# Two value chunks of layer 1 as one Strassen stage, and accumulators that are taken over one by one

## The chip, the cores and the metric

The kernel runs on one core of one Trainium2 chip. The metric is the time of one execution on the device, in microseconds (us); lower is better. Engines are named as in the profile: PE (TensorE), DVE (VectorE), ACT (ScalarE), POOL (GpSimd), SP (SyncE, which here only issues DMAs).

## The reference

Two decoder layers on 256 tokens of width 2048, all in float32. "Layer 1" of the title is `l == 0` in the code: causal attention with 16 heads of 128. With 256 tokens there is one block of 256, so the block-sparse choice selects nothing. Layer 2 attends in a window of 128 with 4 shared K/V heads. Each layer ends with a gated feed-forward of width 5504. Cut to what matters:

```python
# layer 1
q, k, v = jnp.split(x @ w_qkv, 3, axis=-1)          # [256, 2048] @ [2048, 6144]
p = softmax(q k^T * 128**-0.5 + bias[t5_bucket(distance)], causal)   # per head
h = layer_norm(sqrt(2) * x + (p v) @ w_o)
# layer 2: the same with w_kv for 4 heads, w_q, a window of 128 and a learned sink in the softmax
# after each attention
g, u = jnp.split(causal_conv3(h @ w_up) + conv_b, 2, axis=-1)        # width 5504 each
h = layer_norm(sqrt(2) * h + (gelu(g) * u) @ w_down)
```

## The kernel before

**Products in three parts.** Each float32 operand is split into a high part (rounded to the PE's fast float32 form) and a low part (the rest). A product a·b is three matmuls, high·high, high·low and low·high, added in one PSUM bank.

**The weight stream.** All weights come as a list of "halves" of 128x1024 (512 KB), in the order in which PE uses them. SP loads half u into one of six `raw` buffers (L141). ACT makes the high part `wh` (L160), DVE the low part `wl` (L169), each with four buffers. `take` (L204) hands half i to PE and first splits half i+3, whose buffer becomes free when PE has done half i-1; the load of half i+9 is issued when DVE has split half i+3.

**Slots.** `step()` counts one slot for each half. `at(n, f)` puts work n slots ahead; it is issued to ACT, DVE, SP or POOL just before PE's matmuls of that slot and behind that slot's split. Each engine works in its program's order, so an instruction that waits holds up all behind it on that engine. All of the order in this kernel comes from these slots.

**Three ways to multiply.** `ws_unit` (L308) holds weights still and streams all 256 tokens; it makes one 128-wide feature block from two halves. `Moving.chunk` (L405) moves weights of 512 columns past two token tiles: one half is 2 blocks x 2 tiles x 3 = 12 matmuls of 512 columns. Mixed plans (`_mixed`, L62) do part of a projection by Strassen. A quad is 2 blocks of inputs (each 128) x 2 token tiles x 2 chunks of 512 columns; it takes seven products instead of eight. In the plan, `SEVEN` (L51) gives the halves of two quads: B11, B21, B22 are weight blocks, T1 to T4 are sums of weights. A mixed half is 2 products, 6 matmuls.

**Weight sums.** `presums` (L426) makes T1 to T4 ahead of use. For each quad SP loads 1 MB into `gb` in two parts (L433), DVE makes four sums of 128x512 (L436), POOL stores them to DRAM as `ws` (L440), and later they come back as `raw` halves. All quads share one area `gb`, so a quad's load waits for the sums of the quad before it. The first part is loaded in slot m, the second in m+1; the four sums run in slots m+4 to m+7.

**Input sums.** `sums(i)` (L582) makes the sums of inputs that the T halves need, for two quads at a time, in three steps on consecutive slots: `whole`, `combine`, `split` (L588, L599, L604/L605).

**PSUM.** There are eight banks: four named `acc`, four named `at`. In a mixed stage P1, P5, P6, P7 lie in `at`, the outputs (chunk n, token tile t) in `acc`. `evac` adds one output's bank into `res`; a bank can then be taken for another output. `fold` combines P1 to P7.

**Layer 1 attention, the first stage.** For each group g of four heads: the value chunk g (512 columns, `v_group`, 8 halves), then for each head a `ws_unit` for q and one for k, with that head's softmax in slots behind it. That is 4 x (8 + 16) = 96 slots. `project_out` with `PLAN_O` follows: chunks 0 and 1 with four quads (22 halves), chunks 2 and 3 plain (16 halves). `PLAN_DOWN` is the mixed plan of the feed-forward's second product.

**The bias.** The table of biases `ud` is spread into `band` in DRAM by `spread_bias` (L295; 512 KB in rows of 1 KB) and then loaded into `bias` by `load_bias` (L300, on POOL). For layer 1 the four spreads run on POOL, each followed by its load; for layer 2 they are issued by ACT.

Of the kernel before, what the change touches and what calls it, by code (L numbers as in the profile page):

```python
# [2 lines left out]

# [8 lines left out]
F32 = mybir.dt.float32  # L12
# [37 lines left out]
PLAINS_O = (5, 3, 0)  # L50
SEVEN = (("B11", "B21"), ("T1", "T3"), ("T2", "T4"), ("B22", "B22"), ("B11", "B21"), ("T1", "T3"), ("T2", "T4"))  # L51
# [28 lines left out]
ORDER = [q for li in range(4) for q in QUADS[li]]  # L80
AHEAD_OF = {0: QUADS[0] + QUADS[1][:8], 1: QUADS[1][8:] + QUADS[2], 2: QUADS[3][:4], 3: QUADS[3][4:]}
# [7 lines left out]
def _stages():  # L89

    for l in range(2):
        yield [None] * (48 if l else 96), 0
        yield PLAN_O, 2 * l
        yield [None] * (4 * FT), 0
        yield PLAN_DOWN, 2 * l + 1


@with_exitstack
def trunk(ctx: ExitStack, tc: tile.TileContext, wst, wsum, xT_in, x_in, relb, onehot, umask, sinks, conv_in, ln_g, ln_b, out):
# [195 lines left out]
    def spread_bias(l, h0, h1):  # L295
        a = ud[l, h0:h1, :]
        (nc.scalar if l else nc.gpsimd).dma_start(band[l, h0:h1], bass.AP(tensor=a.tensor, offset=a.offset + P - 1,
                                                    ap=[[UL, h1 - h0], [-1, P], [1, 2 * P]]))
# [127 lines left out]
    def presums(quads, first_slot, pitch):  # L426
# [18 lines left out]
        for i, q in enumerate(quads):  # L445
            m = first_slot + pitch * i
# [7 lines left out]
    def project_out(src, plan, li, homes, preload, turnover=None, quad_blocks=None):  # L454

        mv = Moving(src, 0)
        quads = bool(quad_blocks)  # L460
        p0, ns = (NH // 2 - NQ_O, 4) if li % 2 == 0 else (0, 3)
        w0 = nexth["i"] + len(plan) - WINDOW
        n0 = w0 + WINDOW
        after = homes is not None
        if not after:
            aside.update({w0 + j: (xT, j) for j in range(SPARE)})

        def settle():


            ring, places, following = homes()
            aside.update({w0 - len(ring) + j: x for j, x in enumerate(ring) if x})
            aside.update({w0 + j: x for j, x in enumerate(places)})
            aside.update({n0 + 4 + j: x for j, x in enumerate(following)})
            first = w0 - len(ring) - AHEAD
            for i in range(first, w0 + 3):
                reach[i] = i + min(AHEAD + (i - first) * 3 // 5, len(ring) - 1)
            for i, s in enumerate((4, 6, 7, 9, 11, 12, 13), w0 - 4):
                reach[i] = min(max(reach[i], w0 + s), n0 + 5)

        stats = stat.tile([P, 2, NCH, 6], F32, name="stats", bufs=1, padded_shape=[P, 2, NCH, 10])
        gb = gbp.tile([P, 2, D], F32, name="gb")

        def load_gb(i):
            a = (ln_g, ln_b)[i]
            (nc.sync if ns == 3 else nc.gpsimd).dma_start(gb[:, i], bass.AP(tensor=a.tensor, offset=a.offset + li * D, ap=[[0, P], [1, D]]))

        whole = sum(PLAINS[0]) + 7 * (NQ // 2)
        for i in range(2):
            if ns == 3:  # L490
                at((whole - 4, len(plan) - WINDOW - 5)[i], load_gb, i)
            else:
                load_gb(i)
        ag, rs = {}, {}
# [14 lines left out]
        def target(e):  # L509
# [3 lines left out]
            k1, k2, far = src(2 * k), src(2 * k + 1), xsum((k - p0) // 2, ns)  # L513
# [22 lines left out]

        def zs(t, n):
# [552 lines left out]
```

## Time and profile before

| what | value |
|---|---|
| median of 3 runs | 2053.36 us (2053.22 to 2055.54) |
| the profiled execution's own time | 2053.82 us |
| its span (first to last instruction) | 2052.1 us |
| PE busy | 2036.1 us, 99% of the span, 10908 matmuls |
| DVE busy | 1675.9 us, 82% |
| ACT busy | 1138.3 us, 55% |
| POOL busy | 75.4 us, 4% |
| DMA | 566.64 MB, mean 276 GB/s |
| mean granted PE clock | 0.998 |

Matmuls overlap: one of 512 columns lasts 389 ns, but the next starts about 227 ns after it, and that distance is what one costs. In the chain of work that ended last, PE has 98% of the span.

Stages of the profiled execution: group 0's value chunk starts at 5.1 us, group 2's at 151.8 us, group 3's at 225.0 us, layer 1's output projection at 298.3 us.

### The profile page before, as it was taken

The page shows a single profiled execution, that of the slowest core. Times are in us where ns is not written, and L with a number is a line of the kernel's source. Part 1 is how long each engine was busy: PE and PEld are TensorE (multiplying, and loading weights), DVE is VectorE, ACT ScalarE, POOL GpSimd, SP SyncE. Part 2 cuts the span into 40 slices and gives each one's busy share as a digit, 9 for nine tenths or more (in the row PEclk, how much of TensorE's full clock was granted, in tenths as well). Part 3 has the DMA queues.
Part 4 walks back from the last instruction along what each step waited for, and adds up shares of the span by engine and source line. Part 5 has one row for each costly group of instructions (what it writes and reads, how often), then busy time and mean ns, then how long its engine had stood idle before and what let it go on. Part 6 is the DMA issues. An engine that isn't in the chain of part 4 may idle for free.

```text
span 2052.1 us, 29718 instructions
## 1 busy us (share of the span) xinstructions
PE 2036.1 (99%) x10908; PEld 1759.3 (86%) x10908; DVE 1675.9 (82%) x2399; ACT 1138.3 (55%) x1676; POOL 75.4 (4%) x138
## 2 busy tenths in 40 slices
PE   9999999999999999999999999999999999999997
PEld 7888888988888888888888888898888888888886
DVE  5676678888888888899896788978888888889887
ACT  5444456455555555566673556545555555556672
POOL 0100000000000000000000000000000000000000
PEclk9999999999999999999999999999999999999999
DMA  8888988468888888888994767838888888889893
GB/s 297 287 281 328 320 287 313 162 238 282 289 288 273 282 296 269 285 286 329 323 366 156 261 217 252 285 126 275 281 286 283 279 283 291 272 266 328 312 361 150
DMA packets 158722, 566.64 MB, mean 276 GB/s; under 512 B 19008, under 2 KB 21376, under 8 KB 157296
## 3 DMA queue, kind: packets, MB, share of 16 engines
q1 hardware_dynamic: 136064, 492.74, 70.7%
q0 software_dynamic: 20160, 69.64, 8.7%
q10 hardware_dynamic: 2352, 2.36, 0.3%
q8 instruction: 86, 1.41, 0.3%
q14 instruction: 60, 0.49, 0.1%
HBM read 503.78 MB, written 65.06 MB: 277 GB/s over the span
## 4 chain that ended last, share of the span: by engine, by line
PE 98%; DVE 1%; DMA 0%; ACT 0%; issue 0%; ACTq 0%; DVEq 0%
PE acc L322 39%; PE acc L324 20%; PE acc L530 7%; PE acc L531 7%; PE acc L532 7%; PE at L532 2%; PE at L531 2%; PE at L530 2%; PE acc L386 2%; PE acc L385 2%; PE acc L387 2%; PE acc L349 1%; PE acc L361 1%; PE at L722 1%; PE at L755 1%; PE at L748 1%
## 5 line engine op out<-in xcount | busy, mean ns | idle before, releaser
L169 DVE TENSOR_TENSOR wl<-raw,wh 128x1024 fp32r<-128x1024 f32 (+1 forms) x754 | 898.8, 1220 | 186.4 <-ACT wh L160 163.9
L160 ACT ACTIVATE wh<-raw 128x1024 fp32r<-128x1024 f32 (+1 forms) x754 | 770.4, 1052 | 207.9 <-PE acc L532 104.5
L322 PE MATMUL acc<-xT,wh 128*128 128x512 f32 x3456 | 832.8, 392 | 0.0
L322 PEld LDWEIGHTS acc<-xT,wh 128*128 128x128 f32 x3456 | 641.1, 188 | 128.6
L324 PEld LDWEIGHTS acc<-xT,wl 128*128 128x128 f32 x3456 | 444.2, 190 | 12.4
L324 PE MATMUL acc<-xT,wl 128*128 128x256 f32 x3456 | 452.5, 284 | 0.0
L909 ACT ACTIVATE h<-acc 128x256 f32<-128x256 f32 x172 | 66.4, 386 | 409.1 <-PE acc L324 203.1
L917 DVE SCALAR_TENSOR_TENSOR c<-h,cw,c 128x255 f32<-128x255 f32 x344 | 165.4, 481 | 9.1 <-ACT c L913 2.8
L436 DVE TENSOR_TENSOR gb<-gb 128x512 f32<-128x512 f32 x224 | 153.5, 685 | 5.9 <-DMA gb<-in_wsum_dram 5.9
L910 DVE TENSOR_TENSOR h<-acc,h 128x256 f32<-128x256 f32 x172 | 72.7, 423 | 64.2 <-ACT h L909 64.2
L440 POOL DMA_DIRECT2D ws<-gb x112 | 59.8, 534 | 1412.1 <-DVE gb L436 1360.3
L530 PE MATMUL acc<-wh,up 128*128 128x512 f32 x275 | 107.0, 389 | 0.0
L531 PE MATMUL acc<-wl,up 128*128 128x512 f32 x275 | 107.0, 389 | 0.0
L532 PE MATMUL acc<-wh,up 128*128 128x512 f32 x275 | 107.0, 389 | 0.0
L913 ACT ACTIVATE c<-h,cw 128x256 f32<-128x256 f32 x172 | 101.7, 591 | 0.0
L530 PE MATMUL acc<-wh,st 128*128 128x512 f32 x174 | 68.8, 395 | 0.0
L531 PE MATMUL acc<-wl,st 128*128 128x512 f32 x174 | 67.8, 390 | 0.0
L532 PE MATMUL acc<-wh,st 128*128 128x512 f32 x174 | 67.8, 390 | 0.0
L831 ACT ACTIVATE qT<-acc 128x256 f32<-128x256 f32 x32 | 12.3, 385 | 91.3 <-PE acc L324 65.9
L532 PEld LDWEIGHTS acc<-wh,up 128*128 128x128 f32 x275 | 51.6, 188 | 10.7
L530 PEld LDWEIGHTS acc<-wh,up 128*128 128x128 f32 x275 | 51.6, 188 | 10.7
L531 PEld LDWEIGHTS acc<-wl,up 128*128 128x128 f32 x275 | 51.6, 188 | 10.6
(193 smaller groups left out, 2152.5 us busy)
## 6 DMA issues: line engine op xcount, KB each, us to landing
raw<-in_wst_dram SPq DMA_DIRECT2D x694, 512.0 KB, 5.2
gb<-in_wsum_dram SPq DMA_DIRECT2D x112, 512.0 KB, 7.6
ws<-gb POOLq DMA_DIRECT2D x112, 512.0 KB, 6.2
raw<-ws SPq DMA_DIRECT2D x112, 512.0 KB, 5.6
bias<-band POOLq DMA_DIRECT2D x8, 512.0 KB, 7.2
band<-ud POOLq DMA_DIRECT2D x4, 512.0 KB, 12.7
band<-ud ACTq DMA_DIRECT2D x4, 512.0 KB
res<-in_x_dram SPq DMA_DIRECT2D x2, 1024.0 KB, 9.4
```

Source lines behind the costliest of these rows:

```text
L160: nc.scalar.activation(wh[:, c], raws[s][:, c], AF.Copy)
L169: nc.vector.tensor_tensor(out=wl[:, c], in0=raws[s][:, c], in1=wh[:, c].bitcast(F32), op=ALU.subtract)
L322: nc.tensor.matmul(acc, w, xT[:, k, :], start=(k == 0), stop=(k == ends[0]))
L324: nc.tensor.matmul(acc[:, 0:T], w, xT[:, k, 0:T], start=False, stop=(k == ends[1]))
L436: nc.vector.tensor_tensor(out=w[:, o:o + 512], in0=a, in1=b, op=op)
L530: nc.tensor.matmul(acc, sh, wh, start=first, stop=False)
L531: nc.tensor.matmul(acc, sh, wl, start=False, stop=False)
L532: nc.tensor.matmul(acc, sl, wh, start=False, stop=last)
L909: nc.scalar.activation(h, acc[:, T:2 * T], AF.Copy)
L910: nc.vector.tensor_tensor(out=h, in0=acc[:, 0:T], in1=h, op=ALU.add)
L913: nc.scalar.activation(c, h, AF.Identity, bias=w[:, 3:4], scale=w[:, 2:3])
L917: nc.vector.scalar_tensor_tensor(c[:, d:T], h[:, 0:T - d], w[:, 2 - d:3 - d], c[:, d:T], op0=ALU.mult, op1=ALU.add)
```

## The change

1. The value chunks 2 and 3 are made together before group 2 (`v_pair`), by a mixed plan `PLAN_V` with four quads: 5 plain halves, 7 mixed, 3 plain, 7 mixed. Group 3 then has no chunk of its own. The functions of the mixed stages move out of `project_out` into `mixed`, unchanged.
2. The sums of these four quads are made first. Layer 1's attention starts its presums in slot 16 instead of 22 and makes 14 quads instead of 12, one each 6 slots, through the mixed stage too. The feed-forward of layer 1 makes 22 instead of 20, one each 7 slots instead of 8.
3. The bias spreads of layer 1 are issued in slots 4, 6, 8, 10 (before: 4, 9, 14, 19), the last three by ACT instead of POOL. Those of layer 2 move from slots 40, 47, 76, 82 to 76, 82, 88, 94.
4. In all mixed stages an output is evacuated when its own bank is complete, not when both token tiles of the chunk are.

```diff
+PLAN_V = _mixed(1, PLAINS_O, _plain(range(KB - 2 * NQ_O), (2, 3)), KB // 2 - NQ_O)
+QUADS[4] = [(4, 1, KB // 2 - NQ_O + p) for p in range(NQ_O)]
-AHEAD_OF = {0: QUADS[0] + QUADS[1][:8], 1: QUADS[1][8:] + QUADS[2], 2: QUADS[3][:4], 3: QUADS[3][4:]}
+AHEAD_OF = {0: QUADS[4] + QUADS[0] + QUADS[1][:6], 1: QUADS[1][6:] + QUADS[2], 2: QUADS[3][:4], 3: QUADS[3][4:]}
...
     def spread_bias(l, h0, h1):
-        (nc.scalar if l else nc.gpsimd).dma_start(band[l, h0:h1], ...
+        (nc.scalar if l or h0 else nc.gpsimd).dma_start(band[l, h0:h1], ...
...
             for n in range(NCH):
-                if n not in evacuated and done((n, 0), (n, 1)):
-                    evacuated.add(n)
-                    for t in range(2):
-                        at((t + 1) * (n % 2), evac, n, t)
+                for t in range(2):
+                    if (n, t) not in evacuated and done((n, t)):
+                        evacuated.add((n, t))
+                        at(t * (n % 2) * (ns == 3), evac, n, t)
...
-                at(4 + 5 * i, spread_bias, 0, h, h + 4)
-                at((40, 47, 76, 82)[i], spread_bias, 1, h, h + 4)
-            at((4 + 5 * i, 4 * i)[l], load_bias, bias, l, h, h + 4)
+                at(4 + 2 * i, spread_bias, 0, h, h + 4)
+                at((76, 82, 88, 94)[i], spread_bias, 1, h, h + 4)
+            at((5 + 2 * i, 4 * i)[l], load_bias, bias, l, h, h + 4)
...
+        def v_pair():
+            src = lambda k: xT[:, k, :]
+            k0 = KB - 2 * NQ_O
+            vts, begun = {}, set()
...
+            def into(t, n, a):
+                if n not in vts:
+                    vts[n] = pool.tile([P, 2, 512], F32, name="vt", bufs=2)
+                d = vts[n][:, t, :]
+                if (t, n) in begun:
+                    nc.vector.tensor_tensor(out=d, in0=d, in1=a, op=ALU.add)
+                else:
+                    begun.add((t, n))
+                    nc.scalar.activation(d, a, AF.Copy)
+
+            parted = mixed(src, PLAN_V, k0 // 2, 4, lambda i: xT[:, k0 + 4 * i:k0 + 4 * i + 4, :], place, into)
+            mv = Moving(src, 0)
+            for i in range(len(PLAINS_O) - 1):
+                for j, f in enumerate(parted.sums(i)):
+                    at(sum(PLAINS_O[:i]) + 7 * i + j, f)
+            evacuated = set()
+            for half in PLAN_V:
+                blocks = [mv.block() for _ in range(2)]
+                for e, w in zip(half, blocks):
+                    for tgt in parted.target(e):
+                        parted.product(*tgt, *w)
+                step()
+                for n in (2, 3):
+                    for t in range(2):
+                        if (n, t) not in evacuated and parted.done((n, t)):
+                            evacuated.add((n, t))
+                            at(0, lambda n=n, t=t: into(t, n, parted.banks.pop((n, t))))
+            parted.fold(1)
+            run(before)
+            return vts
...
-        presums(AHEAD_OF[2 * l], 3 if l else 22, 8 if l else 6)
+            presums(ahead, [16 + 6 * i for i in range(len(ahead))])
...
-                vt = v_group()
+                if g < 2:
+                    vt = v_group()
+                elif g == 2:
+                    vts = v_pair()
+                if g >= 2:
+                    vt = vts[g]
...
-            presums(AHEAD_OF[2 * l + 1], 4, 8)
+            presums(AHEAD_OF[2 * l + 1], range(4, 158, 8 if l else 7))
```

How the instructions stand, at three places.

DVE before, in the third value chunk (`st` is head outputs, `L` a head's logits, `gb` a weight sum):

```order
L761 TENSOR_TENSOR st<-at,st 128x256
L726 SCALAR_TENSOR_TENSOR L<-at,bias 128x128
L728 TENSOR_REDUCE nm<-L 128x1
L726 SCALAR_TENSOR_TENSOR L<-at,bias 128x256
L728 TENSOR_REDUCE nm<-L 128x1
L169 TENSOR_TENSOR wl<-raw,wh 128x1024
L436 TENSOR_TENSOR gb<-gb 128x512
```

DVE in the changed kernel, from the first mixed group of the pair into the second (`tmp` and `st` are the input sums):

```order
L443 TENSOR_TENSOR gb<-gb 128x512
L176 TENSOR_TENSOR wl<-raw,wh 128x1024
L443 TENSOR_TENSOR gb<-gb 128x512
L176 TENSOR_TENSOR wl<-raw,wh 128x1024
L533 TENSOR_TENSOR tmp<-xT 128x1024
L176 TENSOR_TENSOR wl<-raw,wh 128x1024
L544 TENSOR_TENSOR tmp<-tmp 128x2x128 x4
L176 TENSOR_TENSOR wl<-raw,wh 128x1024
L443 TENSOR_TENSOR gb<-gb 128x512
L550 TENSOR_TENSOR st<-tmp,st 128x1024
L176 TENSOR_TENSOR wl<-raw,wh 128x1024
L443 TENSOR_TENSOR gb<-gb 128x512
```

The weight sums of other quads now stand between the splits of the mixed halves, and one stands ahead of the input sums' last step. In all, four weight sums stand between the split of half 11 and that of half 15, and a fifth ahead of L550.

DVE before, at the end of the mixed part of layer 1's output projection (the `xT` and `up` tiles are here buffers of split weights):

```order
L605 TENSOR_TENSOR xT<-tmp,xT 128x1024
L169 TENSOR_TENSOR wl<-raw,wh 128x1024 x2
L169 TENSOR_TENSOR xT<-raw,xT 128x1024 x3
L169 TENSOR_TENSOR up<-raw,up 128x1024
L549 SCALAR_TENSOR_TENSOR res<-res,acc 128x512
L169 TENSOR_TENSOR up<-raw,up 128x1024
L549 SCALAR_TENSOR_TENSOR res<-res,acc 128x512
L169 TENSOR_TENSOR up<-raw,up 128x1024
L169 TENSOR_TENSOR wl<-raw,wh 128x1024
L549 SCALAR_TENSOR_TENSOR res<-res,acc 128x512 x2
```

The same place in the changed kernel:

```order
L550 TENSOR_TENSOR xT<-tmp,xT 128x1024
L176 TENSOR_TENSOR wl<-raw,wh 128x1024
L613 SCALAR_TENSOR_TENSOR res<-res,acc 128x512
L176 TENSOR_TENSOR wl<-raw,wh 128x1024
L176 TENSOR_TENSOR xT<-raw,xT 128x1024 x2
L613 SCALAR_TENSOR_TENSOR res<-res,acc 128x512
L176 TENSOR_TENSOR xT<-raw,xT 128x1024
L176 TENSOR_TENSOR up<-raw,up 128x1024
L613 SCALAR_TENSOR_TENSOR res<-res,acc 128x512
L176 TENSOR_TENSOR up<-raw,up 128x1024 x2
L176 TENSOR_TENSOR wl<-raw,wh 128x1024
L613 SCALAR_TENSOR_TENSOR res<-res,acc 128x512
```

The first two evacuations move ahead by four to five splits. The banks that they free are those that chunk 2 takes.

SP before, from the end of the inputs' loads to the second quad:

```order
L233 DMA xc<-in_xT_dram 128x512
L141 DMA raw<-in_wst_dram 128x1024 x23
L433 DMA gb<-in_wsum_dram 128x1024
L141 DMA raw<-in_wst_dram 128x1024 x2
L433 DMA gb<-in_wsum_dram 128x1024
```

SP in the changed kernel:

```order
L240 DMA xc<-in_xT_dram 128x512
L148 DMA raw<-in_wst_dram 128x1024 x17
L440 DMA gb<-in_wsum_dram 128x1024
L148 DMA raw<-in_wst_dram 128x1024 x2
L440 DMA gb<-in_wsum_dram 128x1024
```

The first quad's load stands six halves earlier. In the program's semaphores that load now also waits for the landing of the third bias spread that ACT issues, since DMAs of SP and ACT take eight semaphores in turn; before, no load up to slot 40 waited for a spread.

More of the change, by code (lines that the diff above doesn't have):

```diff
@@ L444, in presums @@
                  (1536, b21, w[:, 1024:1536], ALU.subtract))
-        for i, q in enumerate(quads):
-            m = first_slot + pitch * i
+        for m, q in zip(slots, quads, strict=False):
             at(m, load, q, 0)
@@ L452, in presums, with mixed @@
                     at(m + 4 + j, store, q, j // 2)
[L454 to L494, printed above, removed]
+    def mixed(src, plan, p0, ns, quad_blocks, place, into):
         banks, used, owed = {}, {}, {}
@@ L607, in sums, with project_out, settle, load_gb @@
             return whole, combine, split
+        return SimpleNamespace(banks=banks, target=target, product=product, done=done, fold=fold, sums=sums)
+    def project_out(src, plan, li, homes, preload, turnover=None, quad_blocks=None):
+        mv = Moving(src, 0)
+        quads = bool(quad_blocks)
+        p0, ns = (NH // 2 - NQ_O, 4) if li % 2 == 0 else (0, 3)
+        w0 = nexth["i"] + len(plan) - WINDOW
+        n0 = w0 + WINDOW
+        after = homes is not None
+        if not after:
+            aside.update({w0 + j: (xT, j) for j in range(SPARE)})
+        def settle():
+            ring, places, following = homes()
+            aside.update({w0 - len(ring) + j: x for j, x in enumerate(ring) if x})
+            aside.update({w0 + j: x for j, x in enumerate(places)})
+            aside.update({n0 + 4 + j: x for j, x in enumerate(following)})
+            first = w0 - len(ring) - AHEAD
+            for i in range(first, w0 + 3):
+                reach[i] = i + min(AHEAD + (i - first) * 3 // 5, len(ring) - 1)
+            for i, s in enumerate((4, 6, 7, 9, 11, 12, 13), w0 - 4):
+                reach[i] = min(max(reach[i], w0 + s), n0 + 5)
+        stats = stat.tile([P, 2, NCH, 6], F32, name="stats", bufs=1, padded_shape=[P, 2, NCH, 10])
+        gb = gbp.tile([P, 2, D], F32, name="gb")
+        def load_gb(i):
+            a = (ln_g, ln_b)[i]
+            (nc.sync if ns == 3 else nc.gpsimd).dma_start(gb[:, i], bass.AP(tensor=a.tensor, offset=a.offset + li * D, ap=[[0, P], [1, D]]))
+        whole = sum(PLAINS[0]) + 7 * (NQ // 2)
+        for i in range(2):
+            if ns == 3:
+                at((whole - 4, len(plan) - WINDOW - 5)[i], load_gb, i)
+            else:
+                load_gb(i)
+        ag, rs = {}, {}
+        def zs(t, n):
+            return res[:, t, n * 512:(n + 1) * 512]
+        parted = mixed(src, plan, p0, ns, quad_blocks, lambda i: xsum(i, ns), lambda t, n, a: into(t, n, a))
+        banks, target, product, done, fold, sums = (parted.banks, parted.target, parted.product, parted.done, parted.fold,
+                                                    parted.sums)
+        paired = {e[2] for half in plan for e in half if e[0] == "B11"}
+        parts = {(t, n): 1 + (2 if (t, n % 2) == (1, 1) else 1) * (n // 2 in paired) for t in range(2) for n in range(NCH)}
+        scaled = set()
+        def into(t, n, a):
+            z = zs(t, n)
+            if (t, n) in scaled:
+                nc.vector.tensor_tensor(out=z, in0=z, in1=a, op=ALU.add)
+            else:
+                nc.vector.scalar_tensor_tensor(z, z, ALPHA, a, op0=ALU.mult, op1=ALU.add)
+                scaled.add((t, n))
+            parts[t, n] -= 1
+            if not parts[t, n]:
+                nc.vector.bn_stats(stats[:, t, n, :], z)
+        def evac(n, t):
+            into(t, n, banks.pop((n, t)))
```

52 lines of the change are left out of this document (27 added, 25 removed).

## The prediction

> **What bounds the kernel now.** I read the page first: its busy line and the chain of work that ended last.
>
> ```profile
> PE 2036.1 (99%) x10908; PEld 1759.3 (86%) x10908; DVE 1675.9 (82%) x2399; ACT 1138.3 (55%) x1676; POOL 75.4 (4%) x138
> PE 98%; DVE 1%; DMA 0%; ACT 0%; issue 0%; ACTq 0%; DVEq 0%
> ```
>
> PE is the bound almost everywhere. So only two things can shorten the time: fewer matmuls, or the few waits that PE still has. All others can only lengthen it, by making PE wait where it doesn't now. The view of waits, for PE:
>
> ```profile
> PE acc L530 <- DVE res L549: 1.0, 2, 0.5
> PE acc L530 <- DVE res L547: 0.8, 2, 0.4
> PE acc L386 <- DVE wl L169: 0.7, 2, 0.5
> ```
>
> The columns are total us, times, longest. The first two rows are the waits of mixed stages for an evacuation (L547, L549), which the change touches. The third lies in value chunks.
>
> What one matmul costs comes from PE's timeline in the third value chunk, which the change replaces:
>
> ```profile
> 173.41 0.39 PE L385 MATMUL acc<-wh,xT 128*128 128x512 f32 x1
> ...
> 175.91 0.39 PE L387 MATMUL acc<-wh,xT 128*128 128x512 f32 x1
> ```
>
> Eleven matmuls start within 2.50 us: 0.227 us from start to start.
>
> **Part 1, fewer matmuls.** The chunks 2 and 3 have 16 plain halves of 12 matmuls, 192. The pair has 8 plain (96) and 14 mixed of 6 (84), 180. Twelve less, times 0.227: **-2.72 us**, all on PE's path.
>
> **Part 2, one-by-one evacuation.** PE's timeline at the four waits: first the output projection of layer 1, then the first product with `PLAN_DOWN`, then the two of layer 2.
>
> ```profile
> 342.14 0.39 PE L532 MATMUL acc<-xT,st 128*128 128x512 f32 x1
> 343.02 0.50 PE L530 MATMUL acc<-xT,st 128*128 128x512 f32 x1 [0.50 <-DVE res L549]
> ...
> 344.07 0.40 PE L531 MATMUL acc<-xT,st 128*128 128x512 f32 x1
> ```
>
> ```profile
> 982.90 0.39 PE L532 MATMUL acc<-wh,st 128*128 128x512 f32 x1
> 983.67 0.47 PE L530 MATMUL acc<-wh,xT 128*128 128x512 f32 x1 [0.38 <-DVE res L547]
> ...
> 984.44 0.40 PE L530 MATMUL acc<-wh,xT 128*128 128x512 f32 x1
> ```
>
> ```profile
> 1294.27 0.50 PE L530 MATMUL acc<-xT,st 128*128 128x512 f32 x1 [0.49 <-DVE res L549]
> ```
>
> ```profile
> 1934.87 0.47 PE L530 MATMUL acc<-wh,xT 128*128 128x512 f32 x1 [0.38 <-DVE res L547]
> ```
>
> From 342.14 to 344.07 are 1.93 us for five matmuls, 1.14 at their usual distance: 0.80 lost, more than the 0.50 in brackets, since the starts after it are wider apart too. From 982.90 to 984.44 are 1.54 for four (0.91): 0.63. The two of layer 2 have the same brackets, so they count the same: 2 x (0.80 + 0.63) = **-2.86 us**. I take all of it, because the bank that chunk 2 takes is freed four to five splits earlier in the new order of DVE, over 4 us by the 1.14 us of a split (below), and the waits were under 1 us. Bounds: 0, if another bank is late instead, and -2.86. Work late next there is none that PE's waits show.
>
> **Part 3, the pair as a mixed stage with weight sums under it.** This stage has no like in the profile: the output projection is the same plan, but its mixed halves have no weight sums beside them. I take its times and add the sums. PE starts half 5, the first mixed one, here:
>
> ```profile
> 314.37 0.48 PE L530 MATMUL at<-wh,st 128*128 128x512 f32 x1
> ```
>
> Call it T0. From there to half 16 stand seven mixed halves (42 matmuls), three plain (36) and one mixed (6): 84 x 0.227 = 19.07 us. The low part of the second group's input sums is used two matmuls later, at T0 + 19.52 = 333.89. DVE, in three pieces of its timeline:
>
> ```profile
> 294.89 2.36 DVE L169 TENSOR_TENSOR wl<-raw,wh 128x1024 fp32r<-128x1024 f32 x2
> 297.16 0.69 DVE L436 TENSOR_TENSOR gb<-gb 128x512 f32<-128x512 f32 x1
> 297.76 1.22 DVE L169 TENSOR_TENSOR wl<-raw,wh 128x1024 fp32r<-128x1024 f32 x1
> ```
>
> ```profile
> 319.86 6.67 DVE L169 TENSOR_TENSOR wl<-raw,wh 128x1024 fp32r<-128x1024 f32 x5
> 326.44 1.22 DVE L588 TENSOR_TENSOR tmp<-st 128x1024 f32<-128x1024 f32 x1
> ```
>
> ```profile
> 328.02 1.23 DVE L169 TENSOR_TENSOR wl<-raw,wh 128x1024 fp32r<-128x1024 f32 x1 [0.36 <-ACT wh L160]
> ...
> 331.97 1.23 DVE L605 TENSOR_TENSOR xT<-tmp,xT 128x1024 fp32r<-128x1024 f32 x1
> ```
>
> A weight sum costs 297.16 to 297.76, 0.60 us; a split 1.14 (2.36 - 1.22). L605 is done at 333.20, 0.69 before it is needed. In the pair five weight sums stand between the split of half 11 and L605's like: 3.0 us. DVE has room for some of it: the five splits and what follows take 326.44 - 319.86 = 6.58, of which 5 x 1.14 = 5.70 is work, so 0.88 is free, and 0.36 before 328.02. So L605's like comes 3.0 - 0.88 - 0.36 = 1.76 late, less the 0.69 of room: PE waits **1.1 us**. This is what happens if no load is late.
>
> The loads of the weight sums may be. In this stage a half lasts 1.36 us (6 x 0.227) and not the usual 3, so the quad's two loads and its sums lie closer together. Its second part can be issued when DVE has read the same area for the quad before, in my estimate at T0 + 2.6 (behind the split of half 8, which lies between 312.03 and 317.14 in the stage before); the second sum, which reads it, comes behind the split of half 12, at about T0 + 8.3 (319.86 + 2 x 1.14 + 0.60 = 322.7). That leaves 5.7 us for the load. The view of L433 says how long such loads take before:
>
> ```profile
> DMA to landing us min/median/max: 4.4/7.6/10.6
> ```
>
> So DVE waits 0, 1.9 or 4.9 us more, and PE with it: 1.1, 3.0 or 6.0 in all. I take the median, **+3.0**. Lower bound 0: DVE's other work (the stage before also carries the end of a head's softmax) is less than in the row I borrowed from.
>
> The whole stage moves 22 raw halves, 8 loads and 7 stores of weight sums (37 x 0.524 MB) and 1.05 MB of residual: 20.4 MB in the 44 us that the output projection's mixed part takes, 464 GB/s. The best that a window of the profile shows, with the next term's:
>
> ```profile
> 180.00:185.00 5.00, 5.00 (x39) 4.72 (x38) 3.40 (x5) 2.28 (x3) 0.53 (x1) 1.00 1.03 427
> 500.00:600.00 100.00, 100.00 (x576) 88.25 (x575) 84.12 (x132) 55.30 (x90) 4.80 (x9) 1.00 0.83 278
> ```
>
> The last column is GB/s. At 427 the stage's bytes take 47.8 us, 3.8 more than the stage; the ring of loaded halves, which was filled before, is six deep (over 8 us of mixed halves) and covers that, so I count nothing beyond the late loads above. The Trainium skill, "DMA: Bandwidth & Descriptors", section "Where 436 GB/s comes from", says that between HBM and SBUF the HBM side binds, at about 358 GB/s for each core; by it the stage takes 57 us, 13 more than it has, which would leave a PE wait of some 4 us beyond the ring, by my estimate. The row of 427 disagrees, and the measurement decides.
>
> **What I cost at nothing.** The six more halves to load and split, and the 14th quad, lie under PE in layer 1's attention. The feed-forward of layer 1 gets two quads more, 8 sums of 0.69 = 5.5 us of DVE over some 400: in the second window row DVE (third pair) is busy 84 of 100, PE 100. The layer 2 spreads move between slots; SP has waited for them all the same, without any wait of PE there:
>
> ```profile
> SPq L141 <- DMA band<-ud: 16.1, 3, 7.5
> ```
>
> If that cover goes (a wait of over 9 us, three halves of the ring), PE stops. The value tiles' evacuation (ACT, then DVE additions) runs behind the pair, and the units after it take banks freed at halves 15 and 19. ACT is held at slot 6 until `ud` has landed, 28.22 in the next fence, and then issues three spreads; its splits for the first `q` unit come about 3 us later, and it had this much free (3.99 before 35.41):
>
> ```profile
> 35.41 0.38 ACT L831 ACTIVATE qT<-acc 128x256 f32<-128x256 f32 x1 [3.99 <-PE acc L324]
> ```
>
> **Sum.** -2.72 - 2.86 + 3.0 = -2.6. The profiled execution's own time is 2053.82 (its span 2052.1 and 1.7 around it), 0.46 above the median of the runs, 2053.36. So 2051.2 for such an execution, 2050.8 against the median; I say **2051.0**. A difference under 0.2% (4.1 us) can't be told from no change here, so the forecast itself is "same".
>
> **Rival 1, slower: the spreads at the start.** POOL's queue, then the view of L297 for POOL's spreads, and DVE's and the chain's rows where the first sum would stand:
>
> ```profile
> 28.22 1.12 POOL L297 DMA_DIRECT2D band<-ud  x1 [4.44 <-DMA ud<-us]
> 41.51 0.79 POOL L301 DMA_DIRECT2D bias<-band  x1 [12.17 <-DMA band<-ud]
> ```
>
> ```profile
> DMA to landing us min/median/max: 11.5/12.7/14.0
> ```
>
> ```profile
> 66.07 0.42 DVE L832 TENSOR_TENSOR kT<-acc,kT 128x256 f32<-128x256 f32 x1 [1.43 <-ACT kT L831]
> 67.45 2.36 DVE L169 TENSOR_TENSOR wl<-raw,wh 128x1024 fp32r<-128x1024 f32 x2 [0.96 <-ACT wh L160]
> ```
>
> ```profile
> 72.85 0.23 PE acc L322
> 73.08 1.92 PE acc L324 x16
> ```
>
> The first sum's load (slot 16) waits for ACT's third spread to land, and all raw loads stand behind it on SP. Its sum (slot 20) stands ahead of the splits of 67.45, whose result PE needs at 73.08: it can start at 73.08 - 0.69 - 1.22 = 71.2 at the latest. A load that finds the queues empty lands in about 6 (between 4.4 and 7.6), so the third spread must have landed by 65.2. If ACT's spreads begin at 28.8 and run one after the other, that allows 12.1 us each; at 11.5 there's no wait, at 12.7 one of 1.7, at 14.0 one of 5.6. The issues of the same spread by ACT later in the profile, under weight sums, speak for longer: one issued at 146.31 still held SP at 169.18, 22.9 us:
>
> ```profile
> 146.31 0.61 ACTq L297 DMA_DIRECT2D band<-ud  x1
> ```
>
> ```profile
> 169.18 0.90 SPq L141 DMA_DIRECT2D raw<-in_wst_dram  x2
> ```
>
> Against it: at the start no weight sums load the queues. At 15 us each, nearest to the 14.0, the wait is 28.8 + 45 + 6 - 71.2 = 8.6: **2059.6**; it is slower by more than 0.2% (over 2057.5) from 14.3 us each. By the Trainium skill, the same page, section "Why a DMA increments its semaphore by 16 and not by 1", a transfer whose slowest dimension has 4 steps, as a spread's four heads, uses 4 DMA engines, and on ACT's queue always the lowest-numbered, which would put the three spreads on the same four. The 12.7 beside 7.6 for a weight load of the same bytes agrees with the first; no row here shows the second.
>
> **Rival 2, no gain: loads late at their worst.** The 10.6 above: +6.0, so 2053.4 + 0.4 = **2053.8**. The 464 GB/s asked of a peak of 427 speak for it, the ring against it.
>
> **Rival 3, faster: DVE keeps up.** No wait in the pair: -5.6, **2047.8**. For it, the softmax work that isn't in the pair; against it, the five sums that stand where only 1.9 us is free.
>
> **How the numbers follow.** Forecast 0.40 (2049.0 to 2052.5), rival 1 0.25, rival 2 0.15, rival 3 0.20. Faster by over 0.2% is below 2049.2: rival 3, and a seventh of the forecast, 0.26. Slower is above 2057.5: two thirds of rival 1, 0.17. The rest, 0.57, is the same. The range: rival 3's end, 2047.5, to rival 1's price, 2059.6; what lies above has about 0.1 (the longer spreads of rival 1), below 0.08.
>
> **What would show it.** Right: 10896 matmuls; no PE wait at the four places for L547/L549's like; one PE wait of 1 to 6 us at half 16's `T1` product on the input sums' last step, with DVE waiting for `gb` behind half 12's split. Rival 1: a wait of PE for a split near 73 us, SP held until about 74 by a spread. Rival 2: PE waits for splits within the pair on raw loads. Wrong altogether: a wait of PE in a place I have costed at nothing, above all in the feed-forward or under layer 2's spreads.

## The result, and the profile after

The changed kernel takes 2068.38 us (median of 6 runs, 2067.24 to 2069.11) against 2053.98 for the kernel before in the same series. The ratio is 1.0069, 95% interval 1.0056 to 1.0082: 14 us slower. The forecast was 2051.0, which can't be told from no change, with a range that ended at 2059.6; a slower kernel had been given a chance of 0.17. The prediction was wrong.

The page's busy line and chain. The line numbers are those of the changed kernel: L160/L169 of before are L167/L176 here, L530 to L532 are L496 to L498, and L605 is L550.

```profile
PE 2038.4 (99%) x10896; PEld 1759.7 (85%) x10896; DVE 1701.1 (82%) x2441; ACT 1147.4 (56%) x1685; POOL 76.5 (4%) x143
PE 91%; DVE 3%; DMA 3%; issue 1%; ACTq 0%; ACT 0%; SPq 0%; DVEq 0%
```

The twelve matmuls are gone, but the chain now leaves PE for 9% of the span. PE's waits:

```profile
PE acc L331 <- DVE wl L176: 6.0, 2, 4.8
PE at L498 <- DVE st L550: 4.1, 1, 4.1
...
PE at L496 <- ACT st L549: 1.2, 1, 1.2
...
PE at L497 <- DVE wl L176: 0.6, 2, 0.3
```

To size the losses I add up, along PE's timeline, how much farther apart matmuls start than matmuls of the same shapes usually do. That counts waits and slow starts behind them alike, and it closes: the span grew by 13.4 us (2065.5 - 2052.1), and

| place | before | after | change |
|---|---|---|---|
| near 41 to 49 us, first heads | 0 | 7.28 | +7.28 |
| the pair, 196 to 229 us | 0 | 10.48 | +10.48 |
| two output projections, evacuation | 1.53 | 0 | -1.53 |
| two down projections, evacuation | 1.24 | 1.12 | -0.12 |
| twelve matmuls | | | -2.72 |

Nothing else changed by more than tenths. The sizes depend by some tenths on what is taken as the usual distance, and each comes from one profiled execution.

**The start.** ACT's timeline, and PE's at the loss. An ACTq row with a long time is an issue that holds the engine:

```profile
27.85 1.19 ACTq L304 DMA_DIRECT2D band<-ud  x1
29.16 1.06 ACT L167 ACTIVATE wh<-raw 128x1024 fp32r<-128x1024 f32 x1 [3.57 <-issue]
29.19 8.84 ACTq L304 DMA_DIRECT2D band<-ud  x1
...
38.24 8.72 ACTq L304 DMA_DIRECT2D band<-ud  x1
...
47.06 2.00 ACT L167 ACTIVATE wh<-raw 128x1024 fp32r<-128x1024 f32 x2 [6.68 <-issue]
```

```profile
35.54 1.12 PE L331 MATMUL acc<-xT,wl 128*128 128x256 f32 x8
41.42 1.79 PE L331 MATMUL acc<-xT,wl 128*128 128x256 f32 x8 [4.76 <-DVE wl L176]
```

The second and third spread each held ACT almost 9 us. The splits behind them came late, DVE's low parts behind those, and PE waited 4.76 us in the middle of a unit.

**The pair.** PE's timeline:

```profile
194.59 0.39 PE L498 MATMUL acc<-wh,xT 128*128 128x512 f32 x1
196.19 0.50 PE L496 MATMUL at<-wh,st 128*128 128x512 f32 x1 [1.20 <-ACT st L549]
196.52 0.40 PE L497 MATMUL at<-wl,st 128*128 128x512 f32 x1
201.00 0.79 PE L498 MATMUL at<-wh,st 128*128 128x512 f32 x1 [4.08 <-DVE st L550]
201.59 0.63 PE L496 MATMUL at<-wh,st 128*128 128x512 f32 x1
...
205.43 0.50 PE L496 MATMUL acc<-wh,st 128*128 128x512 f32 x1
```

This is the place that was forecast, the low part of the second group's input sums, but PE waits 4.1 us and not 3. Behind it ten matmuls take 4.43 us (201.00 to 205.43) instead of 2.27: PE's granted clock is a half there. The windows of the pair, the last columns PEclk, DMA share, GB/s:

```profile
180.00:190.00 10.00, 10.00 (x46) 8.29 (x45) 8.12 (x10) 6.14 (x6) 0.53 (x1) 1.00 0.99 376
190.00:200.00 10.00, 5.71 (x24) 4.08 (x23) 6.78 (x10) 4.83 (x6) 0.53 (x1) 0.94 1.02 418
200.00:210.00 10.00, 9.01 (x30) 7.27 (x31) 8.95 (x10) 5.00 (x7) 1.07 (x2) 0.72 1.00 351
210.00:220.00 10.00, 8.76 (x54) 7.69 (x53) 6.14 (x8) 5.35 (x8) 0.55 (x2) 1.00 1.01 392
220.00:230.00 10.00, 9.56 (x50) 7.93 (x50) 9.90 (x15) 2.28 (x3) 0.52 (x1) 1.00 1.02 418
```

The DMA engines are busy all the time for 50 us, at 391 GB/s on the mean. Ahead of PE's two waits stand ACT, which waits for a raw load, and DVE, which waits for a load of weight sums:

```profile
194.13 1.06 ACT L167 ACTIVATE wh<-raw 128x1024 fp32r<-128x1024 f32 x1 [3.90 <-DMA raw<-ws]
```

```profile
199.11 0.69 DVE L443 TENSOR_TENSOR gb<-gb 128x512 f32<-128x512 f32 x1 [2.66 <-DMA gb<-in_wsum_dram]
```

So one trace allows two readings: DVE held by a late `gb` load, or every load late. The experiments tell them apart.

### The profile page after: what moved, and what is told of

Same layout as the page of the kernel before. It is cut to its first block, busy times and chain, and to the rows that moved or that the text cites. A ratio compares the mean times of both kernels' runs of the same rounds, so it can differ in the third digit from the quotient of the medians.

```text
span 2065.5 us, 29824 instructions
## 1 busy us (share of the span) xinstructions
PE 2038.4 (99%) x10896; PEld 1759.7 (85%) x10896; DVE 1701.1 (82%) x2441; ACT 1147.4 (56%) x1685; POOL 76.5 (4%) x143
## 4 chain that ended last, share of the span: by engine, by line
PE 91%; DVE 3%; DMA 3%; issue 1%; ACTq 0%; ACT 0%; SPq 0%; DVEq 0%
PE acc L329 37%; PE acc L331 20%; PE acc L496 7%; PE acc L498 7%; PE acc L497 7%; PE at L497 2%; PE at L498 2%; PE at L496 2%; PE acc L356 1%; DMA gb<-in_wsum_dram 1%; DMA raw<-in_wst_dram 1%; DVE wl L176 1%; PE acc L368 1%; PE acc L392 1%; PE acc L393 1%
## 5 line engine op out<-in xcount | busy, mean ns | idle before, releaser
L176 DVE TENSOR_TENSOR wl<-raw,wh 128x1024 fp32r<-128x1024 f32 (+1 forms) x760 | 905.5, 1219 | 180.6 <-ACT wh L167 160.0
L167 ACT ACTIVATE wh<-raw 128x1024 fp32r<-128x1024 f32 (+1 forms) x760 | 776.7, 1052 | 209.8 <-PE acc L498 112.5
L443 DVE TENSOR_TENSOR gb<-gb 128x512 f32<-128x512 f32 x240 | 164.3, 685 | 14.0 <-DMA gb<-in_wsum_dram 14.0
L447 POOL DMA_DIRECT2D ws<-gb x120 | 64.2, 535 | 1418.6 <-DVE gb L443 1343.3
L496 PE MATMUL acc<-wh,up 128*128 128x512 f32 x275 | 107.0, 389 | 0.0
L498 PE MATMUL acc<-wh,up 128*128 128x512 f32 x275 | 107.0, 389 | 0.0
L496 PE MATMUL acc<-wh,st 128*128 128x512 f32 x178 | 70.5, 396 | 0.0
L498 PE MATMUL acc<-wh,st 128*128 128x512 f32 x178 | 69.4, 390 | 0.0
L497 PEld LDWEIGHTS acc<-wl,up 128*128 128x128 f32 x275 | 51.6, 188 | 10.7
L498 PEld LDWEIGHTS acc<-wh,up 128*128 128x128 f32 x275 | 51.6, 188 | 10.7
L496 PEld LDWEIGHTS acc<-wh,up 128*128 128x128 f32 x275 | 51.6, 188 | 10.7
```

Source lines behind the costliest of these rows:

```text
L167: nc.scalar.activation(wh[:, c], raws[s][:, c], AF.Copy)
L176: nc.vector.tensor_tensor(out=wl[:, c], in0=raws[s][:, c], in1=wh[:, c].bitcast(F32), op=ALU.subtract)
L443: nc.vector.tensor_tensor(out=w[:, o:o + 512], in0=a, in1=b, op=op)
L496: nc.tensor.matmul(acc, sh, wh, start=first, stop=False)
L497: nc.tensor.matmul(acc, sh, wl, start=False, stop=False)
L498: nc.tensor.matmul(acc, sl, wh, start=False, stop=last)
```

## The experiments

Losses (in us) at the start (to 110 us) and in the pair are measured as in the table above, in one profiled execution of each kernel; in kernels whose pair is the same they differ by 1 us and more, so differences of that size say little. Ratios are against the kernel before in the same series. The series ran on different chips, so ratios can be compared, medians only within a series.

| kernel | median us | ratio, interval | start | pair |
|---|---|---|---|---|
| spreads apart | 2063.58 | 1.0039 (1.0027 to 1.0051) | 8.4 | 10.6 |
| no loads in the pair | 2059.72 | 1.0024 (1.0016 to 1.0033) | 8.0 | 3.6 |
| no sums in the pair | 2066.32 | 1.0055 (1.0043 to 1.0067) | 7.5 | 9.7 |
| sums that wait for no load | 2066.27 | 1.0056 (1.0044 to 1.0068) | 7.6 | 9.4 |
| before, with one-by-one evacuation | 2052.81 | 0.9994 (0.9985 to 1.0003) | 0 | none |
| start mended | 2060.63 | 1.0028 (1.0016 to 1.0039) | 0 | 13.1 |
| pair relieved, pitch 5 | 2081.86 | 1.0136 (1.0122 to 1.0150) | 4.7 | 0 |
| half spreads (by heads) | 2066.67, one run | | 6.1 | 9.8 |
| one spread | 2061.80 | 1.0032 (1.0019 to 1.0044) | 0.9 | 10.7 |
| one spread, pair relieved | 2051.43 | 0.9981 (0.9972 to 0.9990) | 1.1 | 0 |
| half spreads (by rows) | 2060.73, one run | | 0 | 11.1 |
| one spread, residual later | 2059.06 | 1.0018 (1.0009 to 1.0027) | 0 | 8.7 |

**The pair: loads, sums, or the wait between them.** Three edits of the changed kernel, with `hot = (52, 58, 64)`, the slots of the three quads under the mixed halves. The products that use these sums are then not those of the reference; the work and its order on the engines are what is timed. No loads:

```diff
-            at(m, load, q, 0)
-            at(m + 1, load, q, 1)
+            if m not in hot:
+                at(m, load, q, 0)
+                at(m + 1, load, q, 1)
```

> The changed kernel without the loads of the weight sums of slots 52, 58 and 64 (six loads of 512 KB; the sums there use what lies in the buffer, so the products that use them are not those of the reference). PE lost 10.5 us in the pair. Theory: DVE waits for late loads of gb, and what stands behind it on DVE is late for PE; a part of it is the half clock after PE's wait. Then nearly all is gone: 2058 us. Rival, the raw loads are late because the queues are full: also nearly all gone, since six of some 37 transfers are missing. Rival, DVE simply has too much work: 3 us of the loss or more stay, 2061 or more.

No sums:

```diff
-                at(m + 4 + j, step_of, *x)
+                if m not in hot:
+                    at(m + 4 + j, step_of, *x)
```

> The changed kernel without DVE's twelve weight sums of slots 56 to 59, 62 to 65 and 68 to 71 (loads and stores stay, so the traffic is the same; the products that use these sums are not those of the reference). Theory, late gb loads hold DVE: DVE waits for none of them, 2059 us, with the 1.5 us near 196 left, where ACT waits for a raw load. Rival, the queues are full and the raw loads late: half of the 10.5 us or more stays, 2063 or more. Rival, DVE has too much work: all gone, 2058.

Sums that wait for no load:

```diff
-                at(m + 4 + j, step_of, *x)
+                own = w[:, x[0]:x[0] + 512]
+                at(m + 4 + j, step_of, *((x[0], own, own, ALU.add) if m in hot else x))
```

> The changed kernel with the same loads, the same twelve sums and the same stores, but the sums of slots 56 to 71 add an area to itself that no load writes, so DVE has its work and waits for no load (these sums are not those of the reference). Theory, late gb loads hold DVE: 2060 us, 8 of the 10.5 us gone. Rival, too much work for DVE: 3 us or more of a wait for the input sums stays near 200 us, with a half clock behind it, 2064 or more. Rival, raw loads late: PE's waits move to splits whose raw loads are late, 2063 or more.

Without the loads 6.9 of the 10.5 us went (or more: its profiled execution was the longest of ten, 2061.90 against a median of 2059.72). Without the sums, or with sums that wait for no load, less than 1.2 went. So my first theory, DVE held by late `gb` loads, fell, and so did "too much work for DVE". ACT's rows at the same place, first without the sums, then with unbound ones, show what was left:

```profile
197.79 1.06 ACT L167 ACTIVATE wh<-raw 128x1024 fp32r<-128x1024 f32 x1 [5.15 <-DMA raw<-ws]
```

```profile
194.94 1.06 ACT L167 ACTIVATE wh<-raw 128x1024 fp32r<-128x1024 f32 x1 [4.39 <-DMA raw<-ws]
```

The same half's raw load is late in both. In the changed kernel the raw loads issued from 176 to 200 us landed after 10.8 us in the median; without the loads of weight sums it was 7.4, without the sums 16.5. Without the sums the queues are as full as before, and the clock falls as far:

```profile
190.00:200.00 10.00, 5.10 (x23) 3.91 (x21) 6.14 (x8) 3.75 (x4) 0.00 (x0) 0.98 1.02 419
200.00:210.00 10.00, 9.77 (x29) 7.17 (x30) 4.92 (x5) 4.54 (x5) 0.00 (x0) 0.68 1.01 377
```

**The start: spreads apart.**

```diff
-                at(4 + 2 * i, spread_bias, 0, h, h + 4)
+                at(4 + 5 * i, spread_bias, 0, h, h + 4)
...
-            at((5 + 2 * i, 4 * i)[l], load_bias, bias, l, h, h + 4)
+            at((5 + 5 * i, 4 * i)[l], load_bias, bias, l, h, h + 4)
```

> The changed kernel, with the layer 1 spreads at slots 4, 9, 14, 19 (the three of ACT five slots, some 15 us, apart instead of two). Theory: PE lost 7.3 us near 41 to 49 us because ACT's second and third spread were issued while the first was still running and each held ACT for 8.8 us; apart, an issue takes about 1 us and those 7.3 us are gone: 2061 us. Rival: ACT's spreads are slow to issue beside the weight loads at this place however far apart: each still holds ACT about 8 us, and the time stays near 2068. Second rival: what counts is that SP waits for a spread to land (8.2 us in the changed kernel); then the waits of PE turn up later, at 70 to 90 us, and the time is 2064 or more.

The runs lay between 2059.7 and 2068.1. ACT's issues were short again (1.19, 0.61 and 0.61 us), and the loss at 41 us was gone. In the profiled execution, the longest of them, another came instead. POOL's queue, and DVE's timeline:

```profile
83.84 0.76 POOL L308 DMA_DIRECT2D bias<-band  x1 [18.98 <-DMA band<-ud]
```

```profile
95.06 0.69 DVE L443 TENSOR_TENSOR gb<-gb 128x512 f32<-128x512 f32 x1 [5.82 <-DMA ws<-gb]
```

POOL waited for the last spread, and the stores of weight sums stood behind. DVE's next sum writes the area that they read, so DVE waited, and PE lost 7.2 us at 96 us. So the theory held for ACT, and of the second rival the outcome: PE's wait turned up later, though through POOL and not through SP. With the spreads as far apart, and the bias loads out of the way as well:

```diff
-                at(4 + 2 * i, spread_bias, 0, h, h + 4)
+                at(4 + 5 * i, spread_bias, 0, h, h + 4)
...
-            at((5 + 2 * i, 4 * i)[l], load_bias, bias, l, h, h + 4)
+            at(((5, 18, 40, 46)[i], 4 * i)[l], load_bias, bias, l, h, h + 4)
```

> The changed kernel with the spreads at slots 4, 9, 14, 19 and their loads at 5, 18, 40, 46, so that ACT issues no spread while one is running and POOL, which also stores the weight sums, waits for no spread while stores are due. Theory: the 7.3 us at the start go and no wait of DVE for a store comes instead; the loss in the pair (10.5) stays: 7 us less than the changed kernel, about 1.003 of the kernel before. Rival: spreads that run beside weight sums hold SP or POOL anyway, and 3 us or more are lost between 50 and 110 us.

The start lost nothing, and the time is as expected. The loss in the pair was 13.1 in the profiled execution, which was the longest of seven (2063.31 against a median of 2060.63).

**What held ACT.** Half spreads by heads (two heads of 128 rows), then by rows (four heads of 64); in both, the second halves follow in slots 14, 19 and 24, and the last three bias loads move to slots 23, 40 and 46. By heads:

```diff
-                at(4 + 2 * i, spread_bias, 0, h, h + 4)
+                at(4 + 2 * i, spread_bias, 0, h, h + (2 if i else 4))
...
```

By rows:

```diff
-                at(4 + 2 * i, spread_bias, 0, h, h + 4)
+                at(4 + 2 * i, spread_bias, 0, h, h + 4, 0, P // 2 if i else P)
...
```

> The changed kernel with each spread of ACT cut in two: the first halves (256 rows of 1 KB) at slots 6, 8 and 10 as before, the second halves at slots 14, 19 and 24; loads of the bias at slots 5, 23, 40, 46. How long the second and the third issue hold ACT tells why. Theory, a limit on rows outstanding: in the changed kernel ACT came free when about 1.4 and 1.7 spreads were outstanding, by the landing of the first; three halves are 1.5, so the second is issued in about 1 us and the third in less than 2. Rival, ACT waits until the transfer before it is done: each holds it 4 us or more.

> The changed kernel with each ACT spread cut by rows: four heads, 64 rows each, at slots 6, 8, 10 (so the same engines as the whole spread, half the rows for each), the rest at slots 14, 19, 24. Theory, rows outstanding for each engine: the second issue finds 64 rows ahead and not 128, so it is held less than 3 us, and the third about half of the 8.7 us or less. Rival, ACT waits until the transfer before it has ended: the second is held as long as half a spread lasts, 5 to 6 us, and the third as well.

ACT's three issues by heads, and by rows:

```profile
27.83 1.19 ACTq L304 DMA_DIRECT2D band<-ud  x1
29.16 8.45 ACTq L304 DMA_DIRECT2D band<-ud  x1
37.82 7.69 ACTq L304 DMA_DIRECT2D band<-ud  x1
```

```profile
27.25 1.18 ACTq L304 DMA_DIRECT2D band<-ud  x1
28.58 0.58 ACTq L304 DMA_DIRECT2D band<-ud  x1
35.32 3.52 ACTq L304 DMA_DIRECT2D band<-ud  x1
```

Both have the same 256 rows in each transfer. By heads my expectation of the count of all rows fell: half the rows held ACT nearly as long as the whole. By rows the second issue wasn't held, straight behind the first, and the third 3.5 us. Nor does ACT wait until the transfer before has ended: in the changed kernel its second issue was over at 38.0, while POOL's load of the first spread waited for it until 43.9. So what counts here is not rows in all, but how many rows each head has in them. The Trainium skill, "DMA: Bandwidth & Descriptors", section "Why a DMA increments its semaphore by 16 and not by 1", says that a transfer uses as many DMA engines as the largest number up to 16 that divides its slowest dimension: 4 for a spread, 2 for a half by heads, so 128 rows for each engine in both, and 64 by rows. These runs agree with it: behind 128 rows, 128 more hold ACT 7.7 us or longer; behind 64 rows, 64 more don't. No row here shows the engines of a spread themselves, so that the rows of one engine are the cause is argued, not shown.

If all rows counted, one transfer of twelve heads would hold ACT longest; by the rows of each head, nothing stands before it:

```diff
-                at(4 + 2 * i, spread_bias, 0, h, h + 4)
-                at((76, 82, 88, 94)[i], spread_bias, 1, h, h + 4)
+                if i < 2:
+                    at(4 + 2 * i, spread_bias, 0, h, (4, NH)[i])
+                if i == 0:
+                    at(76, spread_bias, 1, 0, NH)
```

> The changed kernel with ACT's three spreads of four heads made as one transfer of twelve heads in slot 6 (for layer 2 one of sixteen heads in slot 76). In the changed kernel a second transfer held ACT 8.8 us, and 8.45 when it had half the rows but also (by the Trainium skill, the page on DMA bandwidth and descriptors, a transfer takes as many engines as its outermost dimension allows) half the engines. Theory: what holds ACT is the rows that wait for one engine, 128 with either; a first transfer never waits, however many engines, so one of twelve heads is issued in about 1.2 us, the start loses nothing, and it lands near 45 us instead of 68. Then 7 us less than the changed kernel: 2061 us, ratio 1.003. Rival: issuing time goes by all rows; 1536 rows hold ACT 20 us or more, and the time is 2075 or more.

ACT's issue and POOL's three loads behind it:

```profile
27.36 1.36 ACTq L304 DMA_DIRECT2D band<-ud  x1
```

```profile
50.82 2.26 POOL L308 DMA_DIRECT2D bias<-band  x3 [7.76 <-DMA band<-ud]
```

1536 rows were issued in 1.36 us, so the count of all rows fell again. They had landed by 50.8 (expected: near 45), against 68.4 for three spreads one behind the other. The time came out as expected.

**The evacuation alone**, put into the kernel before:

```diff
-                if n not in evacuated and done((n, 0), (n, 1)):
-                    evacuated.add(n)
-                    for t in range(2):
-                        at((t + 1) * (n % 2), evac, n, t)
+                for t in range(2):
+                    if (n, t) not in evacuated and done((n, t)):
+                        evacuated.add((n, t))
+                        at(t * (n % 2) * (ns == 3), evac, n, t)
```

> The kernel before with the one-by-one evacuation alone. The prediction's term: -2.86 us. Theory from the trace of the changed kernel: the two waits at the output projections go (0.77 and 0.76), but those of the feed-forwards' second products are only replaced by a wait of 0.56 for a split that now stands behind an evacuation (0.62 before): -1.65 us.

The median fell by 1.46 us, with an interval that holds no change. The trace gives -1.65: the waits at both output projections are gone, and in the down projections one for a split has taken their place:

```profile
986.40 0.50 PE L531 MATMUL at<-wl,xT 128*128 128x512 f32 x1 [0.29 <-DVE wl L169]
```

**The pair without other traffic.** First beside the mended start:

```diff
-AHEAD_OF = {0: QUADS[4] + QUADS[0] + QUADS[1][:6], 1: QUADS[1][6:] + QUADS[2], 2: QUADS[3][:4], 3: QUADS[3][4:]}
+AHEAD_OF = {0: QUADS[4] + QUADS[0] + QUADS[1][:3], 1: QUADS[1][3:] + QUADS[2], 2: QUADS[3][:4], 3: QUADS[3][4:]}
...
-        at(55 + 15 * t, load_residual, t)
+        at(73 + 10 * t, load_residual, t)
...
-            presums(ahead, [16 + 6 * i for i in range(len(ahead))])
+            presums(ahead, [16, 21, 26, 31, 36, 41, 71, 76, 81, 86, 91])
...
-            presums(AHEAD_OF[2 * l + 1], range(4, 158, 8 if l else 7))
+            presums(AHEAD_OF[2 * l + 1], range(4, 158, 8 if l else 6))
...
```

> The same mended start, and the pair freed of other traffic: eleven quads in layer 1's attention at slots 16 to 41 (pitch 5) and 71 to 91, none of whose loads or stores fall among the mixed halves, three more quads in the feed-forward (pitch 6), and the residual's loads in slots 73 and 83. Theory, the pair lost its 10.5 us because more was asked of the queues than the 420 GB/s that they moved: no loss in the pair, so only the gains stay, -2.72 - 1.65 = -4.4 us against the kernel before (0.9979). Rival, the pair's mixed halves alone ask too much (22 halves of 512 KB in some 41 us, 280 GB/s on the mean, but 385 GB/s in the mixed halves of 1.36 us): 2 to 4 us stay. Rival, the three quads more in the feed-forward make DVE late there: slower than before.

The pair lost nothing, but the kernel was 28 us slower. A pitch of five is too short: a quad's first load then stands ahead of the last two sums of the quad before, in the same area, so some of its sums are of other data, and DVE, loads and stores wait for each other all through the attention (6.8 us at 119, 4.1 at 153, 6.3 at 263). The kernel is no test of the time, only of the pair. With a pitch of six and the one spread, nine quads are made in layer 1's attention and 27 in its feed-forward:

```diff
-AHEAD_OF = {0: QUADS[4] + QUADS[0] + QUADS[1][:6], 1: QUADS[1][6:] + QUADS[2], 2: QUADS[3][:4], 3: QUADS[3][4:]}
+AHEAD_OF = {0: QUADS[4] + QUADS[0] + QUADS[1][:1], 1: QUADS[1][1:] + QUADS[2], 2: QUADS[3][:4], 3: QUADS[3][4:]}
...
-        at(55 + 15 * t, load_residual, t)
+        at(73 + 10 * t, load_residual, t)
...
-            presums(ahead, [16 + 6 * i for i in range(len(ahead))])
+            presums(ahead, [16, 22, 28, 34, 40, 70, 76, 82, 88])
...
-            presums(AHEAD_OF[2 * l + 1], range(4, 158, 8 if l else 7))
+            presums(AHEAD_OF[2 * l + 1], range(4, 158, 8) if l else range(4, 164, 6))
...
```

> The same one spread, and the pair freed of other traffic with the quads at the pitch of six that the shared area needs: nine quads in layer 1's attention (slots 16 to 40 and 70 to 88), 27 in its feed-forward (pitch 6), the residual's loads in slots 73 and 83. Theory, the pair's loss is traffic: no loss there, and -4.4 us against the kernel before, ratio 0.998. Rival, the pair's own 22 halves with 14 short ones ask too much already: 2 to 5 us stay, no faster than before. Rival, 27 quads make DVE late in the feed-forward: slower than before.

This one beats both kernels: 4.0 us below the kernel before by medians (2051.43 against 2055.44), 0.19% with an interval of 0.10 to 0.28%. Its windows in the pair have a full clock and room in the queues:

```profile
180.00:190.00 10.00, 10.00 (x45) 8.28 (x45) 9.05 (x11) 5.86 (x7) 0.00 (x0) 1.00 0.85 319
190.00:200.00 10.00, 10.00 (x45) 8.26 (x44) 8.82 (x8) 7.91 (x10) 0.00 (x0) 1.00 0.90 299
```

DVE is busier here than in the changed kernel (8.9 of 10 us against 8.0, the mean of the three windows from 180 to 210), and PE waits for none of it. How long the raw loads issued from 176 to 200 us took, first in the changed kernel, then in this one:

```profile
DMA to landing us min/median/max: 10.3/10.8/11.9
```

```profile
DMA to landing us min/median/max: 3.2/5.6/6.4
```

**The residual's share**, with the one spread:

```diff
-        at(55 + 15 * t, load_residual, t)
+        at(73 + 10 * t, load_residual, t)
```

> The kernel with one spread, and the residual's two loads (1 MB each, one of them among the pair's mixed halves) moved from slots 55 and 70 to 73 and 83; the weight sums stay under the pair. The pair lost 10 to 11 us with both, 0 with neither, and 3.6 us with the residual but without the six loads of weight sums. Theory, every transfer counts alike by its bytes: 1 MB of the 20.4 MB is 2.5 us at 420 GB/s, so 6 to 8 us of loss stay, ratio about 1.002. Rival, the residual's load counts for more since it stands in SP's queue ahead of the raw loads of the sums: 4 us or less stay, ratio 1.0005 or less.

8.7 us stay of 10.7, a little more than the 6 to 8 expected, and the ratio is as expected. 1 MB less in the pair is 2.0 us less, where its bytes alone would be 2.5. One trace of each can't tell these two figures apart, but the rival (4 us or less) fell.

This trace also shows the half clock without a long wait. PE's timeline, and the window around it:

```profile
189.76 0.50 PE L496 MATMUL at<-wh,st 128*128 128x512 f32 x1 [1.54 <-ACT st L549]
190.10 0.40 PE L497 MATMUL at<-wl,st 128*128 128x512 f32 x1
192.23 0.79 PE L498 MATMUL at<-wh,st 128*128 128x512 f32 x1 [1.74 <-DVE st L550]
192.82 0.63 PE L496 MATMUL at<-wh,st 128*128 128x512 f32 x1
```

```profile
190.00:200.00 10.00, 8.26 (x25) 6.25 (x25) 8.48 (x10) 5.51 (x7) 1.07 (x2) 0.66 1.03 397
```

## Why the prediction was wrong

- **Matmuls, -2.72:** right; 10896 matmuls, and the account closes with it.
- **Evacuation, -2.86:** mis-sized, -1.65. The step that failed is "Work late next there is none that PE's waits show". In the down projections an evacuation is followed by its statistics (1.4 us of DVE in all), and now both stand ahead of a split that PE needs. DVE's timeline and PE's wait in the changed kernel:

```profile
998.29 0.68 DVE L611 TENSOR_TENSOR res<-res,acc 128x512 f32<-128x512 f32 x1
999.01 0.69 DVE L617 BATCH_NORM_STATS2 stats<-res 128x6 f32<-128x512 f32 x1
```

```profile
1000.88 0.50 PE L497 MATMUL at<-wl,xT 128*128 128x512 f32 x1 [0.29 <-DVE wl L176]
```

- **The pair, +3.0:** 10.5. The place was right, and the trace even has the sign that was named: DVE waits 2.66 us for `gb`, then PE 4.1 us for L550. But as the cause of the loss the mechanism was wrong. I priced a DVE queue with one late load in it, and without that wait (unbound sums) 9.4 us stayed, without the sums 9.7. The step that failed is "I count nothing beyond the late loads": I set 464 GB/s of demand against the best window of 427, took 3.8 us of lag from it and let the ring of loads cover that. But a window's best rate isn't what a crowded stage gets: the pair's windows had 391 on the mean. By that, 20.4 MB take 52 us against 44. The ring, some 8 us of mixed halves, would still have covered most of that, so the rate alone doesn't explain the loss. What the ring had to cover is each raw load's own time, and that was 10.8 us in the median there, against 5.6 in the relieved kernel. It isn't the whole account either: with the residual later it was 7.6, and 8.7 us of loss stayed. That the loads are the cause is shown by moving them; how the loss follows from their lateness is argued. A late raw load also holds all that stands behind it on ACT and DVE, the input sums among it. The Trainium skill's 358 GB/s ("DMA: Bandwidth & Descriptors", section "Where 436 GB/s comes from"), which I set aside for the 427, gave 57 us and, by my estimate, 4 us of wait. The measured rate lies between the two, and the loss was above what either gave.
- **What the estimate had no term for:** the clock. With PE's waits of 4 to 5 us came a stretch of matmuls at half the granted clock, 2.2 us lost by it in the pair. Such a wait costs more than its length here. The Trainium skill, "TensorE: Matmul & The Clock Gate", section "HAM oscillation — how this bites in real kernels", has the rule: gaps of PE over about 3.4 us bring its clock down. The waits of 4.1 and 4.8 us here agree, but shorter ones did it too: with one spread and the residual later, waits of 1.54 and 1.74 us, 0.7 us apart, came with a granted clock of 0.66 over 10 us (above). A single wait of 2.6 us with unbound sums (at 227 us) did not. So the length of one wait doesn't decide it here; what does wasn't tried.
- **The start, at nothing:** +7.3, the step that failed outright. The three spreads that ACT "then issues", with "its splits for the first `q` unit" coming "about 3 us later", were taken at about 1 us each, as one that is alone. The second and third took 8.8 and 8.7. Before, ACT's spreads lay some 20 us apart, so the trace couldn't show two behind each other, and I gave no bounds for it.
- **Rival 1** named the spreads, but another mechanism. SP did wait for the third to land, at 68, later than the 65.2 that I allowed:

```profile
SPq L440 <- DMA band<-ud: 8.2, 1, 8.2
```

```profile
73.93 0.69 DVE L443 TENSOR_TENSOR gb<-gb 128x512 f32<-128x512 f32 x1
```

The first sum then waited for nothing, since PE and DVE were by then some 7.5 us behind themselves. At 73.9 it ran some 3 us later than the 71.2 that I allowed; whether that would have cost PE anything in a start that lost nothing wasn't tried by itself.
- **Rival 2** (loads late) named the raw loads as its sign, which is the mechanism of the pair, and priced it at 6.0 of the 10.5. **Rival 3** is what the relieved kernel comes near: -4.0 against -5.6, and 1.2 of the difference is the evacuation's term.

## What to carry to other kernels

Compare a stage's bytes with the rate that a crowded stretch sustains, not with the best window, and count every transfer in it, also those for later stages. If they don't fit, move them: here the same work at another place, with the three spreads in one transfer, turned +0.7% into -0.2%. Before a DMA moves to a compute engine's queue, ask what it costs if the one before it is still running: an issue that is short alone can hold the engine for 9 us, and all its splits behind it. When a wait is removed by putting work earlier, look at what that work now stands ahead of.

## What the hardware showed that was not expected

- An ACT-issued transfer of 1 KB rows is issued in 0.6 to 1.4 us when the one before was issued 13 us or more earlier, however large (1536 rows over twelve heads: 1.36). It takes 7.7 to 8.8 us straight behind one with the same 128 rows for each of its heads. With only 64 rows a head the second took 0.58 and the third 3.52.
- Three spreads in one transfer landed in about 23 us (27.4 to 50.8), three single ones in 40 (27.9 to 68.4).
- With a wait of PE of over 4 us, matmuls of 512 columns started 0.43 us apart instead of 0.227 for over 4 us (granted clock 0.72 over 10 us). The same came with two waits of 1.54 and 1.74 us (0.66 over 10 us), but not with one of 2.6.
- Weight loads of 512 KB that landed in 5.6 us with the DMA engines 85 to 90% busy took 10.8 us in a stretch with them busy all the time.
